# A soft mixture-of-experts product with two and three levels of fast matrix multiplication: products regrouped in pairs, more pairs split a third time, VectorE planned by other durations

## The chip, the cores and the metric

The kernel runs on one core of a Trainium2 chip. The metric is device time in microseconds (us) of one execution, from the host's view of the device; the profiler's span, from the first to the last instruction, is a little shorter. TensorE (PE) multiplies, VectorE (DVE) adds, subtracts and multiplies elementwise, ScalarE (ACT) copies, GpSimd (POOL) and SyncE (SP) do almost nothing here but start transfers (DMAs); ACT starts some too. Each of these engines works through its own queue in the order in which the program put the instructions there.

## What is computed

Every token gets a weight for each of 8 experts by a softmax, and the output is the weighted sum of the experts' products:

```
batch, seq, hidden, n_experts, expert_hidden = 16, 512, 512, 8, 2048
probs = softmax(router_logits)                       # [16, 512, 8]
for e in range(n_experts):
    output += probs[:, :, e:e+1] * np.matmul(x, expert_weights[e])
```

With the weights multiplied into x this is one product: 8192 tokens by a depth of 8 x 512 = 4096, times 4096 by 2048.

## The kernel before

**Three levels.** The product is split by Winograd's form of Strassen's scheme: seven half-size products in place of eight, for some additions of blocks. On the outer level tokens come in 16 pairs q of 256-token blocks (2q and 2q+1), the depth in two halves of 4 experts and the columns in two halves of 1024. The seven outer products are called 1, 2, 5, 6, 7, 4, 3 here (P1, P2, ...), in the order in which the kernel goes through them; each runs over all q (P1 from q = 2 on; what it would give for q = 0 and 1 is computed directly at the start). On the inner level each outer product is split again into seven **steps**, `STEPS = (1, 5, 6, 2, 7, 3, 4)`, each of 128 tokens, depth 1024 and 512 columns: eight matmuls of 512 columns. On the third level, in a **third** stage, the steps 1 and 5 of two outer products of one kind are taken together (256 tokens, depth 1024, 512 columns) and split into seven parts of four matmuls of 256 columns each, twice: 56 matmuls of 256 columns in place of 32 of 512.

**Stages and slots.** `stages` is a list of one or two outer products that run interleaved, step by step; a stage of two has 14 **slots** of one step each (`SLOT = 1.73`, the us that the plan takes for one). Stages 0 to 14 hold P1 and P2, `k5` = 15 is the first of P5. `run(stage)` goes through them; in a third stage `run_third` first runs the 14 parts, with the last two slots of the stage before put between them (`held`), and then slots 4 to 13. `at(stage, slot, ...)` hangs work on a slot: casts and fetches of weights, fetches of bases.

**What a step needs.** A left operand (`Left`): x times the probabilities, for both halves of depth (`times`, one DVE operation of 128x2048 each, written to a z tile), a difference `s2` (128x1024) and a difference `i` (128x2048). A right operand (`Right`): seven blocks of 1024 x 512 weights, of which four (5, 6, 7, 4) are differences (128x4096 on DVE). In a third stage four more sums `s` per stage (128x1024) and, once per kind of product, eight differences `t` of weights (`Split`, 128x1024 each). After a step the result leaves PSUM: `post_alone` (P1, P5, P3: two of seven copies add on DVE, the others are ACT copies) or `post_on_base` (P2, P6, P7, P4: six of seven add on DVE to a base already in an `h` tile). In a third stage there are four more half-width additions on DVE and four half-width copies on ACT, two of which write a temporary `t5` in an `h` tile.

**The order of DVE.** DVE's order is written out while the program is built. `later(cost, make)` appends an operation to one first-in-first-out `queue`; `slack()` after every slot advances a clock of PE by `SLOT` and takes operations from the queue as long as DVE's own clock is `LAG` = 0.3 behind it; `need` takes everything up to an operation that the next step needs; `evacuated` puts in an addition that reads PSUM. The costs are 0.69, 1.22, 2.29 and 0.42 us for 1024, 2048, 4096 columns and the half-width addition. At slot 1 of a stage the left operands of the next one are queued (`queue_lefts`), at its start the `i` of its own.

**Loads.** `start_loads(s + 2)` at slot 1 of stage s starts the loads of x and of the probabilities (`pT`), `finish_loads(s + 2)` at slot 7 turns x that was read for the first time (`xs`, cast by POOL) by four DMA transposes on SP's queue; its transposed form is stored for later use (`x_dram`, read back as `xT<-x`). `xpool` has 10 tiles of 2 KB per partition for these, `hpool` 12 tiles of 2 KB for outputs, bases and `t5`, `wpool` 15 tiles of 8 KB for weights, `t`, `s` and weights being prepared. P1's results for q go to `kept` in DRAM and are read again as P6's base, and as P2's where they are not in `h` tiles any more.

**Stages 0 to 14 before.** Four pairs of P1 (q = 2 to 9), six mixed stages of P2 with q = 9 to 14 and P1 with q = 10 to 15, five pairs of P2 (15, 0 to 8). Stages 2, 3 (P1) and 11 (P2) are third stages, and six of P3 at the end. In mixed stages P2 with q >= 9 takes its base and its transposed x from the tiles that P1 left.

**Weights for later.** `b21` is block 21 of the weights, cast in stages 0 to 2, from which P2's operands are made in stage 3. T blocks (`t1`, `t2`, `t3`: differences of blocks 11, 12 and 22) are made for three of four (k, n) by `wedge`, from `b11` in SBUF and two casts, in six halves in stages 4 to 9, and for `ODD` = (0, 1) by `odd_t` from three whole casts. They go to DRAM, `t1` and `t2` come back for P5 and P6.

**The end.** The last stage holds one product, P3 with q = 13, as `finish`, with steps 1, 5, 6, 7, 3, 4, 2; step 2 is computed in two halves of 256 columns at the very end, the first copied by DVE, the second by ACT.

Of the kernel before, what the change touches and what calls it, by code (L numbers as in the profile page):

```python
# [31 lines left out]
def kernel(  # L32
# [34 lines left out]
    xpool = ctx.enter_context(tc.tile_pool(name="xpool", bufs=10))  # L67
    hpool = ctx.enter_context(tc.tile_pool(name="hpool", bufs=12))
# [304 lines left out]
    def evacuated(cost=0.69):  # L373
        clock["dve"] = max(clock["dve"], clock["pe"]) + cost
# [51 lines left out]
    class Left:  # L426
# [31 lines left out]
        def queue_make(self, k):  # L458
            for make in self.makes(k):
                self.task[k] = later(1.22, make)  # L460

        def queue_s2(self):
# [3 lines left out]
            self.task["s2"] = later(0.69, make)  # L466

        def queue_i(self):
# [5 lines left out]
            self.task["i"] = later(1.22, make)  # L474
# [19 lines left out]
    class Right:  # L494
# [9 lines left out]
        def queue_sum(self, sums, p):  # L504
            self.task[p] = later(2.29, sums[p])
# [66 lines left out]
    class Split:  # L572
# [5 lines left out]
        def queue(self):  # L578
            for p in THIRD:
                for i in range(4):  # L580
                    self.task[p, i] = later(0.69, lambda p=p, i=i: self.make(p, i))
# [18 lines left out]
    class Third:  # L600
# [5 lines left out]
        def queue_sums(self):  # L606
            for i in range(4):
                self.task.append(later(0.69, lambda i=i: self.make(i)))
# [17 lines left out]
        def part(self, p, m):  # L626
# [14 lines left out]
            elif m in (6, 7):  # L641
                evacuated(0.42)
# [41 lines left out]
    right[1] = Right(w, {p: Task(2.29, sums[p]) for p in (6, 7, 4)})  # L684
# [33 lines left out]
    def product(r, q, **how):  # L718
# [7 lines left out]
        elif r == 2:  # L726
            if q >= 9:
# [111 lines left out]
    def run(stage):  # L839
# [3 lines left out]
        slots = [(p, i) for i in range(len(STEPS)) for p in some]  # L843
# [54 lines left out]
    def joined(q, tn):  # L898
        m1 = bases[6, q]
        m1.task[tn] = later(0.69, lambda: tt(m1.t[tn], m1.t[tn], products[5, q].o[tn], SUB), True)  # L900
# [40 lines left out]
    def wedge_at(stage, slot, kn, e, then):  # L941
# [7 lines left out]
        def go_on():  # L949
            for make in made:  # L950
                later(1.22, make)
# [8 lines left out]
    for i, kn in enumerate(((0, 0), (0, 1), (1, 1), (1, 0))):  # L960
        at((11 * i + 8) // 14, (11 * i + 8) % 14, lambda kn=kn: cast21(kn))
# [8 lines left out]
    sums_at(3, 3, 2, b21, (5,))  # L970
    sums_at(3, 5, 2, b21, (6,))
    sums_at(3, 7, 2, b21, (7,))
    sums_at(3, 12, 2, b21, (4,))
    for i, (kn, e) in enumerate((kn, e) for kn in ((0, 0), (1, 0), (1, 1)) for e in range(2)):
        wedge_at(4 + i, 2, kn, e, (4 + i, 11))
# [9 lines left out]
    def cast_odd(q):  # L985
        made[q] = cast_block(q, ODD)

    def odd_t():

        def make1():  # L990
            t1[ODD] = made[11]
            tt(t1[ODD], made[11], made[12], SUB)
# [221 lines left out]
```

## Time and profile before

| | us |
|---|---|
| median of 3 runs | 1382.1 |
| lowest, highest | 1379.82, 1384.07 |
| profiled execution, its time | 1378.23 |
| profiled execution, its span | 1376.5 |
| POOL queue's transfers | 185.12 MB |
| SP queue's transfers | 130.15 MB |
| ACT queue's transfers | 42.08 MB |

The profile is one execution on the chip. Times in its views are from the span's start. An instruction's duration includes its passage through the engine's pipeline, so that in a busy engine the next one starts before the first has ended; where the text speaks of **spacing** it means the difference of two starts. A number in brackets at the end of a row is the idle time of the engine before that instruction and what ended it. Almost every instruction goes through a helper, so rows are told apart by their tiles: `ps<-w,z` is an ordinary step, `ps<-w,d` is step 6, `ps<-t,s`, `ps<-w,s` and `ps<-t,z` are parts of the third level, `z<-xT,pT` makes a left operand, `z<-z,d` is an `i`, `h<-ps,h` an addition that empties PSUM.

### The profile page before, as it was taken

How to read it: one execution, taken by the hardware profiler on the slowest of the kernel's cores; microseconds unless marked ns; L12 is line 12 of the kernel's file. 1: busy time of each engine (PE TensorE's matmuls, PEld its weight loads, DVE VectorE, ACT ScalarE, POOL GpSimd, SP SyncE). 2: the span in 40 equal slices, each digit the busy share in tenths (PEclk: the TensorE clock that was granted, in tenths of full speed). 3: DMA queues.
4: the chain of work that ended last, by engine and by line, in shares of the span. 5: the costliest groups of instructions: out<-in, count | busy, mean ns of one | idle time of the engine just before them, and what ended most of it. 6: DMA issues, size and time to landing. Idle time of an engine off the chain costs nothing.

```text
span 1376.5 us, 18061 instructions
## 1 busy us (share of the span) xinstructions
PE 1363.1 (99%) x6610; PEld 643.8 (47%) x6610; DVE 1125.8 (82%) x1360; ACT 193.3 (14%) x353; POOL 411.4 (30%) x652
## 2 busy tenths in 40 slices
PE   8999999999999999999999999999999999999998
PEld 4455444445444444444444444444444444456554
DVE  5877767678989888789897878888889898987875
ACT  3222111100001111111111100000000000123221
POOL 3122333231222243343242112232332422232222
PEclk9999999999999999999999999999999999999999
DMA  9999899999897999999999898888797969999886
GB/s 180 199 258 219 214 233 279 236 315 340 252 327 237 321 308 315 295 318 320 334 286 307 327 399 237 194 236 211 227 266 203 259 188 310 289 225 239 211 184 117
DMA packets 193161, 358.50 MB, mean 260 GB/s; under 512 B 53168, under 2 KB 87216, under 8 KB 187696
## 3 DMA queue, kind: packets, MB, share of 16 engines
q0 software_dynamic: 88688, 185.12, 55.7%
q1 hardware_dynamic: 98336, 130.15, 31.1%
q10 hardware_dynamic: 6048, 42.08, 8.0%
q8 instruction: 51, 0.84, 0.2%
q14 instruction: 38, 0.31, 0.1%
HBM read 214.47 MB, written 170.07 MB: 279 GB/s over the span
## 4 chain that ended last, share of the span: by engine, by line
PE 69%; issue 11%; DMA 11%; POOL 5%; DVE 3%; SPq 1%; ACT 0%; POOLq 0%; DVEq 0%; ACTq 0%
PE ps L132 69%; POOL out_dram L126 3%; DMA out_dram<-h 3%; DMA wd<-w 2%; DMA w<-in_expert_weights_dram 2%; DMA w<-wd 2%; DMA xT<-xs 1%; POOL wd L126 1%; DMA pT<-p_dram 1%; SPq L397 1%; DVE h L112 1%; POOL w L126 1%; DVE z L112 1%; DVE s L112 0%; POOL xs L126 0%
## 5 line engine op out<-in xcount | busy, mean ns | idle before, releaser
L132 PE MATMUL ps<-w,z 128*128 128x512 f16 (+1 forms) x5272 | 1136.0, 376 | 3.8 <-DMA w<-in_expert_weights_dram 1.9
L132 PEld LDWEIGHTS <-z 128*128 128x128 f16 x5344 | 522.6, 98 | 609.6 <-issue 2.5
L126 POOL DMA_DIRECT2D out_dram<-h x380 | 248.6, 660 | 724.1 <-ACT h L559 352.2
L112 DVE TENSOR_TENSOR h<-ps,h 128x512 f32<-128x512 f32 x415 | 284.7, 688 | 175.0 <-PE ps L132 147.0
L112 DVE TENSOR_TENSOR z<-xT,pT 128x2048 f16<-128x2048 f16 x220 | 266.8, 1218 | 12.1 <-DMA xT<-xs 10.0
L132 PE MATMUL ps<-w,d 128*128 128x512 f16 x880 | 199.1, 379 | 1.2 <-DMA w<-wd 1.2
L132 PEld LDWEIGHTS <-d 128*128 128x128 f16 x880 | 86.1, 98 | 103.3 <-issue 1.5
L112 DVE TENSOR_TENSOR z<-z,d 128x2048 f16<-128x2048 f16 x110 | 132.3, 1217 | 0.0
L112 DVE TENSOR_TENSOR w<-w 128x1024 f16<-128x1024 f16 (+2 forms) x92 | 101.0, 1103 | 5.9 <-DMA wd<-w 3.4
L559 ACT COPY h<-ps 128x512 f32<-128x512 f32 x64 | 37.5, 586 | 482.9 <-PE ps L132 414.2
L548 ACT COPY h<-ps 128x512 f32<-128x512 f32 x90 | 52.7, 586 | 325.6 <-PE ps L132 304.6
L112 DVE TENSOR_TENSOR ps<-ps,h 128x512 f32<-128x512 f32 (+1 forms) x102 | 60.6, 599 | 31.9 <-PE ps L132 31.8
L112 DVE TENSOR_TENSOR d<-z 128x1024 f16<-128x1024 f16 x110 | 74.8, 686 | 2.0 <-PE ps L132 0.7
L545 ACT COPY h<-ps 128x512 f32<-128x512 f32 x90 | 52.0, 589 | 151.7 <-PE ps L132 146.6
L126 POOL DMA_DIRECT2D w<-in_expert_weights_dram x65 | 48.4, 761 | 38.6 <-DMA wd<-w 28.3
L126 POOL DMA_DIRECT2D wd<-w x86 | 48.2, 584 | 37.1 <-DVE w L112 28.9
L126 POOL DMA_DIRECT2D kept<-h x56 | 30.8, 550 | 73.8 <-ACT h L548 41.1
L112 DVE TENSOR_TENSOR z<-z,u 128x2048 f16<-128x2048 f16 x38 | 46.4, 1221 | 0.6
L112 DVE TENSOR_TENSOR u<-xT,pT 128x2048 f16<-128x2048 f16 x38 | 46.3, 1217 | 0.0
L112 DVE TENSOR_TENSOR h<-h 128x512 f32<-128x512 f32 (+2 forms) x69 | 45.2, 676 | 0.4 <-DMA h<-kept 0.3
L541 ACT COPY ps<-ps 128x512 f32<-128x512 f32 x45 | 25.6, 570 | 104.5 <-PE ps L132 99.4
L112 DVE TENSOR_TENSOR z<-z 128x2048 f16<-128x2048 f16 x32 | 39.1, 1222 | 0.6
(61 smaller groups left out, 262.5 us busy)
## 6 DMA issues: line engine op xcount, KB each, us to landing
out_dram<-h POOLq DMA_DIRECT2D x380, 256.0 KB, 6.7
pT<-p_dram SPq DMA_DIRECT2D x127, 256.0 KB, 6.3
w<-wd ACTq DMA_DIRECT2D x27, 1024.0 KB, 9.4
h<-kept SPq DMA_DIRECT2D x100, 256.0 KB, 7.1
xT<-x SPq DMA_DIRECT2D x74, 256.0 KB, 6.6
wd<-w POOLq DMA_DIRECT2D x72, 256.0 KB, 6.7
w<-in_expert_weights_dram POOLq DMA_DIRECT2D x35, 512.0 KB, 9.9
h<-out_dram SPq DMA_DIRECT2D x68, 256.0 KB, 4.8
```

The source lines that it names most:

```text
L112: dve(nc.vector.tensor_tensor(out=o, in0=a, in1=b, op=op))
L126: note(nc.gpsimd.dma_start(out=o, in_=i, **how))
L132: note(nc.tensor.matmul(ps, z, w, start=start, stop=stop, skip_group_check=True))
L397: note(nc.sync.dma_start_transpose(out=self.t[:, :, ds(j * P, P)], in_=self.xs[:, j, :]))
L541: act(nc.scalar.copy(self.banks["b"], x))
L545: act(nc.scalar.copy(o[tn], q if p == 5 else x))
L548: act(nc.scalar.copy(o[TN[p]], b if p == 2 else x))
L559: act(nc.scalar.copy(o[tn], b))
```

## The change

The stages 0 to 14 become seven pairs of P1 (q = 2 to 15) and eight of P2 (14 and 15, then 0 to 13), none mixed. Third stages are 2 to 6 (P1) and 8 to 11 (P2), nine where there were three; those of P3 stay. P2 takes base and x from the tiles of P1 for q = 14 and 15 alone. The casts of `b21` move to stages 3 to 5, P2's operands are made in stage 6. `wedge` makes T blocks for (0, 0) and (1, 0) in stages 1 to 5, during P1; for (1, 1) `odd_t` makes them in stages 7 to 9, during P2, from three whole casts, and `t1` of it stays in SBUF. DVE is planned with 0.61, 1.14, 2.2 and 0.35. `xpool` has 9 tiles and `hpool` 13. In the last stage step 3 stands before 7, and step 4 between the halves of step 2; both halves are copied by ACT.

```
-    xpool = ctx.enter_context(tc.tile_pool(name="xpool", bufs=10))
-    hpool = ctx.enter_context(tc.tile_pool(name="hpool", bufs=12))
+    xpool = ctx.enter_context(tc.tile_pool(name="xpool", bufs=9))
+    hpool = ctx.enter_context(tc.tile_pool(name="hpool", bufs=13))
...
-    def evacuated(cost=0.69):
+    def evacuated(cost=0.61):
...
-                self.task[k] = later(1.22, make)
+                self.task[k] = later(1.14, make)
...
-            self.task[p] = later(2.29, sums[p])
+            self.task[p] = later(2.2, sums[p])
...
-                evacuated(0.42)
+                evacuated(0.35)
...
-            if q >= 9:
+            if q >= 14:
                 base = products[1, q].o.__getitem__
...
-    for q in (2, 4, 6, 8):
+    for q in range(2, 16, 2):
         add(product(1, q), product(1, q + 1))
-    for q in range(9, 15):
-        add(product(2, q), product(1, q + 1))
-    forget(*range(0, 18, 2))
-    rest = [15] + list(range(9))
-    for i in range(0, 10, 2):
+    k2 = len(stages)
+    forget(*range(0, 28, 2))
+    rest = [14, 15] + list(range(14))
+    for i in range(0, 16, 2):
         k = add(product(2, rest[i]), product(2, rest[i + 1]))
         for slot, tn in zip((8, 10, 12, 13), INNER):
             for q in rest[i:i + 2]:
-                if q < 9:
+                if q < 14:
                     fetch_at(k if tn == (1, 0) else k - 1, 3 if tn == (1, 0) else slot, bases[2, q], tn)
...
-    for i, kn in enumerate(((0, 0), (0, 1), (1, 1), (1, 0))):
-        at((11 * i + 8) // 14, (11 * i + 8) % 14, lambda kn=kn: cast21(kn))
+    for where, kn in zip([(3, 10), (4, 7), (5, 4), (5, 13)], ((0, 0), (0, 1), (1, 1), (1, 0))):
+        at(*where, lambda kn=kn: cast21(kn))
...
-    sums_at(3, 3, 2, b21, (5,))
+    sums_at(k2 - 1, 3, 2, b21, (5,))
...
-    for i, (kn, e) in enumerate((kn, e) for kn in ((0, 0), (1, 0), (1, 1)) for e in range(2)):
-        wedge_at(4 + i, 2, kn, e, (4 + i, 11))
+    for (kn, e), (where, then) in zip(((kn, e) for kn in ((0, 0), (1, 0)) for e in range(2)), [((1, 2), (1, 13)), ((2, 4), (3, 1)), ((3, 6), (4, 3)), ((4, 8), (5, 5))]):
+        wedge_at(*where, kn, e, then)
...
+    for q, where in zip((12, 11, 22), [(7, 4), (7, 10), (8, 2), (8, 12)]):
+        at(*where, lambda q=q: cast_odd(q, (1, 1)))
+    at(*(8, 12), lambda: odd_t((1, 1)))
     for i, kn in enumerate(((0, 0), (1, 1), (1, 0))):
-        fetch_at_w(11 + (8 + 4 * i) // 14, (8 + 4 * i) % 14, t1, "t1", kn)
+        if kn != (1, 1):
+            fetch_at_w(11 + (8 + 4 * i) // 14, (8 + 4 * i) % 14, t1, "t1", kn)
...
-    finish.steps = (1, 5, 6, 7, 3, 4, 2)
+    finish.steps = (1, 5, 6, 3, 7, "2a", 4, "2b")
...
-    for stage in (2, 3):
+    for stage in [2, 3, 4, 5, 6]:
         third(stage, 1)
-    at(1, 2, splits[1].queue)
-    for stage in (11,):
+    at(1, 0, splits[1].queue)
+    for stage in [8, 9, 10, 11]:
         third(stage, 2)
-    at(10, 2, splits[2].queue)
+    at(k2, 2, splits[2].queue)
```

`splits[r].queue` puts the eight differences `t` into DVE's queue: before at slot 2, behind the next stage's left operands that come at slot 1; for P1 now at slot 0, ahead of them.

More of the change, by code (lines that the diff above doesn't have):

```diff
@@ L683 @@
     right = {r: Right() for r in (2, 5, 6, 7, 4, 3)}
-    right[1] = Right(w, {p: Task(2.29, sums[p]) for p in (6, 7, 4)})
+    right[1] = Right(w, {p: Task(2.2, sums[p]) for p in (6, 7, 4)})
     lefts, xs, ps_, bases = {}, {}, {}, {}
@@ L842, in run @@
             p.left.queue_i()
-        slots = [(p, i) for i in range(len(STEPS)) for p in some]
+        slots = [(p, i) for i in range(len(some[0].steps)) for p in some]
         def one(n):
```

82 lines of the change are left out of this document (44 added, 38 removed).

## The prediction

> **What bounds the kernel now.** I read the page's head first, then who PE waited for, then the order of time on PE, then DVE, ACT and SP around each place where PE stood.
>
> ```profile
> span 1376.5 us, 18061 instructions
> PE 1363.1 (99%) x6610; PEld 643.8 (47%) x6610; DVE 1125.8 (82%) x1360; ACT 193.3 (14%) x353; POOL 411.4 (30%) x652
> ...
> PE ps L132 <- DVE t L112: 1.3, 1, 1.3
> PE ps L132 <- DMA w<-wd: 1.2, 1, 1.2
> ```
>
> PE is the bound; it waits for single microseconds in single places. So the time falls if PE gets fewer columns, or if those places go, and rises if a cover breaks.
>
> ```profile
> 1153.03 3.62 PE L132 MATMUL ps<-w,d 128*128 128x512 f16 x16
> 1156.48 20.88 PE L132 MATMUL ps<-w,z 128*128 128x512 f16 x96
> 1177.20 3.62 PE L132 MATMUL ps<-w,d 128*128 128x512 f16 x16
> ...
> 1223.01 1.04 PE L132 MATMUL ps<-w,s 128*128 128x256 f16 x8
> ...
> 1224.76 3.62 PE L132 MATMUL ps<-w,d 128*128 128x512 f16 x16
> 1248.14 2.11 PE L132 MATMUL ps<-w,d 128*128 128x512 f16 x9
> ...
> L132 PEld LDWEIGHTS <-s 128*128 128x128 f16 x288 | 28.1, 98 | 8.4 <-issue 2.1 <-DVE s L112 1.3
> ```
>
> Step 6 (`ps<-w,d`) comes once per stage, so it is a ruler. An ordinary stage takes 1177.20 - 1153.03 = 24.17 us (16 matmuls 3.45, so 0.216 each), a third stage 1248.14 - 1224.76 = 23.38 (16 matmuls of 256 columns from 1223.01 on take 1.75, so 0.109 each, with the weight loads, 98 ns, hidden beside them). Check: 32 x 0.216 = 6.9 against 56 x 0.109 = 6.1, difference 0.8.
>
> **Six more third stages** (five of P1 for two, four of P2 for one; P3's six stay). Each saves 24.17 - 23.38 = 0.79: 6 x 0.79 = **-4.7 us**. It is PE's own work, so nothing hides it.
>
> The Trainium skill speaks against it: "TensorE: Matmul & The Clock Gate", section "Back-to-back issue gap", has the sustained spacing set by the weight load as well, 81 ns at 128 columns and 131 at 512. A straight line between gives an estimate of 98 at 256 columns, and then a third stage would cost 56 x 98 - 32 x 131 = 1.3 us instead of saving. The rows above disagree (109 and 216 ns).
>
> **The first third stage** (2, in both kernels).
>
> ```profile
> 74.73 3.62 PE L132 MATMUL ps<-w,d 128*128 128x512 f16 x16
> ...
> 79.34 1.23 DVE L112 TENSOR_TENSOR z<-xT,pT 128x2048 f16<-128x2048 f16 x1 [7.44 <-DMA xT<-xs]
> ...
> 86.74 0.69 DVE L112 TENSOR_TENSOR t<-w 128x1024 f16<-128x1024 f16 x1
> ...
> 91.34 2.76 PE L132 MATMUL ps<-w,z 128*128 128x512 f16 x16 [0.73 <-DVE h L112]
> ...
> 99.61 3.62 PE L132 MATMUL ps<-w,d 128*128 128x512 f16 x16
> ```
>
> DVE stood 7.44 us for a transposed x, and only then, at 86.74, came to the eight `t` that the third level needs; PE lost 1.5 by the ruler (99.61 - 74.73 = 24.88, less 23.38), half of it before 91.34. Queued at slot 0, the `t` (8 x 0.6 = 4.8) go into that 7.44. I take **-1.1**; bounds 0 (the x is later still) and -1.5. The wedge now at slots 2 and 13 of stage 1 is queued behind the next left operands, so it delays stage 3, which has room.
>
> **The first third stage of P2** (11 before, 8 after) shows what can go wrong four times.
>
> ```profile
> 292.21 3.62 PE L132 MATMUL ps<-w,d 128*128 128x512 f16 x16
> ...
> 293.80 0.69 DVE L112 TENSOR_TENSOR h<-ps,h 128x512 f32<-128x512 f32 x1 [2.94 <-DMA kept<-h]
> ...
> 300.94 2.36 DVE L112 TENSOR_TENSOR z<-xT,pT 128x2048 f16<-128x2048 f16 x2
> 303.21 0.69 DVE L112 TENSOR_TENSOR h<-ps,h 128x512 f32<-128x512 f32 x1
> 303.81 0.69 DVE L112 TENSOR_TENSOR t<-w 128x1024 f16<-128x1024 f16 x1
> ...
> 308.00 0.69 DVE L112 TENSOR_TENSOR t<-w 128x1024 f16<-128x1024 f16 x1
> 308.75 0.60 PE L132 MATMUL ps<-t,s 128*128 128x256 f16 x4 [1.26 <-DVE t L112]
> 311.86 0.60 PE L132 MATMUL ps<-w,z 128*128 128x256 f16 x4 [0.35 <-ACT ps L638]
> 311.16 0.37 ACT L640 COPY h<-ps 128x256 f32<-128x256 f32 x1 [3.66 <-DMA out_dram<-h]
> ...
> 317.51 3.62 PE L132 MATMUL ps<-w,d 128*128 128x512 f16 x16
> ```
>
> Spacings: 0.60 for 1024 columns and for an addition from PSUM (303.21 to 303.81), 2.27/2 = 1.13 for 2048. The new costs 0.61 and 1.14 are these; the old ones were 8 to 15% over. PE lost 317.51 - 292.21 - 23.38 = 1.9 here, for two things. First, the fifth `t` ended at 308.7. From the stage's start (292.21 less four slots, 285.3) DVE owes 2 `i` (2.3), 10 additions (6.0), 4 left halves (4.5), 4 `s` and 2 `s2` (3.6) and 5 `t` (3.0), in all 19.4, against 12 slots of 1.73 plus the parts ahead of it, 22.0; the idle 2.94 for a store that had not landed, with 0.5 for PE, used the room up. Secondly `t5` found all 12 `h` tiles taken and waited 3.66 for an output to land, with the next ACT copy behind it.
>
> In stage 7 DVE owes the same 19.4. The wait for `kept<-h` should shrink: stage 6 has no output stores and no weight casts ahead of it on POOL's queue. The 13th `h` tile gives the first `t5` its place, so the next ACT copy is not stuck. I put the stall at 0.7 (bounds 0 and 1.9), a gain of **-1.2**. Stages 8 to 10 owe from third to third 12 additions (7.2), 4 half-width ones (1.7 by the old plan's cost), 2 `i` (2.3) and 8.1 of left operands and sums, 19.3 of 23.4; 1.8 of late `t` and then 6.6 of `odd_t` (3 x 2.2, row below) come on top. `odd_t` is queued behind stage 10's left operands, so stage 9 is asked for 25.9 and about 2.5 spill into 10, 21.8 of 23.4: full, not over.
>
> ```profile
> 137.67 2.28 DVE L112 TENSOR_TENSOR w<-w 128x4096 f16<-128x4096 f16 x1
> 139.87 2.35 DVE L112 TENSOR_TENSOR z<-z,d 128x2048 f16<-128x2048 f16 x2
> ```
>
> "VectorE: DVE Perf Modes" of the Trainium skill, section "The DRAIN you can't avoid", lets the next operation start only when the pipeline is empty. By durations these stages would owe a tenth more and stage 9 would miss its end; starts 0.60 apart for 0.69 long say otherwise.
>
> **The end.**
>
> ```profile
> 1363.57 1.89 PE L132 MATMUL ps<-w,d 128*128 128x512 f16 x8
> ...
> 1365.50 0.69 DVE L112 TENSOR_TENSOR h<-ps,h 128x512 f32<-128x512 f32 x1 [1.03 <-DMA out_dram<-h]
> 1366.24 7.09 PE L132 MATMUL ps<-w,z 128*128 128x512 f16 x40 [0.78 <-DVE h L112]
> ```
>
> Alone in its stage, step 7 goes on in the bank that step 6 just filled, and waits for DVE to read it: 1366.24 - 1363.57 - 8 x 0.216 = 0.95. With step 3 (1.73) between, that read is covered. Step 4 has half of step 2 (0.87) between it and 7; a read of about 0.95 leaves 0.1. **-0.85**, bounds 0 and -0.95. The tail behind the last matmul is an ACT copy and its store in both: 0.
>
> **The new plan of DVE** holds for all stages. It pulls operations up to 8% earlier, into gaps such as this:
>
> ```profile
> 1327.17 0.69 DVE L112 TENSOR_TENSOR h<-ps,h 128x512 f32<-128x512 f32 x1 [1.82 <-issue]
> 1332.97 0.69 DVE L112 TENSOR_TENSOR s<-z 128x1024 f16<-128x1024 f16 x1
> 1333.71 0.61 PE L132 MATMUL ps<-t,s 128*128 128x256 f16 x4 [1.02 <-DVE s L112]
> ```
>
> Here DVE idled 1.82 and PE then lost 1.0. I count half, **-0.5**, bounds -1.0 and, where an operation pulled forward waits for its load with additions behind it, a loss of up to the 2.94 seen above. The price of an addition that comes up to 0.84 later (one 1.14 operation less LAG) is nothing in a stage of two, where a bank is next used three slots (5.2) on.
>
> **Loads and buffers.** P2's base and x for five more q are read back: 20 x 256 KB and 5 x 256 KB; the block 11 cast for (1, 1) replaces a store and a fetch of `t1`. They cost PE nothing while they land a stage ahead. A tile less in `xpool` bounds SP:
>
> ```profile
> SPq L123 <- DVE z L112: 414.5, 55, 21.1
> ...
> 889.59 1.81 SPq L123 DMA_DIRECT2D h<-out_dram  x4
> 891.45 0.42 SPq L123 DMA_DIRECT2D pT<-p_dram  x1
> 895.76 0.33 SPq L123 DMA_DIRECT2D xT<-x  x1
> ```
>
> SP issues when DVE releases a tile, two at a time here. With nine, each load takes the release after: nothing to speak of inside a couple, 4.3 us (891.45 to 895.76) across; the bases issued between shift by the same, and loads run a stage (24) ahead. P1's pairs turn two new x per stage for seven stages instead of four, with `b21` casts and wedges beside them in 3 to 5:
>
> ```profile
> 67.80:92.70 24.90, 24.17 (x120) 11.62 (x119) 15.97 (x22) 6.53 (x13) 5.16 (x8) 1.00 1.19 248
> 188.60:212.80 24.20, 24.20 (x114) 10.99 (x113) 16.75 (x20) 3.50 (x6) 8.22 (x15) 1.00 1.03 250
> ```
>
> The next to last column, the DMA share, is higher where two x are turned (1.19) than where one is (1.03). What more it costs no row shows. From below it is 0; from above the 7.44 wait of DVE, repeated in four stages against some 7 us of room (x came at 79.34 and, without the `t`, would have served until about 87), so 0 to 3 each. I take **+1.9** for this, for P2's full stages and for waits the new order brings.
>
> Sum: -4.7 - 1.1 - 1.2 - 0.85 - 0.5 + 1.9 = **-6.5**. The profiled execution took 1378.23 (span 1376.5 and 1.7 around it), so 1371.7 by its measure; the median of the three runs is 3.9 higher, 1382.1, and I state the forecast against that: **1375.6**.
>
> **Rivals.** (B) *Every P2 third stage stalls as stage 11 did*, 1.9 each: 7.6 instead of 0.7. For it: four full DVE stages, `h` tiles wanted 14 to 13. Against: half of that loss was a late store, and the 13th tile. 1375.6 + 6.9 = 1382.5: no change.
> (C) *P1's transposes fall behind*: two x per stage, one tile less and the casts beside them, so that from stage 3 on x lands later than some 9 us before the third stage begins. DVE waits first in line with wedge and sums behind it; 3 us in each of stages 3 to 6, 12 less the 1.9 already counted: 1385.7, slower; and P2's operands in stage 6 come late as well. Against: `b21` no longer competes in stages 0 to 2, and P1 asks DVE for 14.5 of 23.4 (4 left halves 4.5, 2 `i` 2.3, 2 `s2` and 4 `s` 3.6, 4 additions 2.4, half-width ones 1.7).
> (D) *The third level costs rather than saves*, where weight loads don't hide: 56 x (109 + 98) = 11.6 us against 32 x (216 + 98) = 10.0, so +1.6 for -0.79, six times: 1375.6 + 14.3 = 1389.9, slower. For it: the load is nine tenths of a 256-column matmul. Against: the third stages of P3 ran at 23.4. That is the way of the page on TensorE named above; the trace bears it out nowhere.
> (E) *The waits are many small ones*: 5.9 in place of my 1.9, of the kinds in B and C. 1379.6, no change to measure.
>
> **Chances.** Forecast 0.60, E 0.13, B 0.10, C 0.15, D 0.02. A difference under 0.3% (4.1 us) can't be told from none. Of the forecast's 0.60, 0.08 gains less than that; of E 0.05 and of B 0.03 gain more; of C 0.03 loses less. Faster 0.60 - 0.08 + 0.05 + 0.03 = 0.60; slower 0.15 - 0.03 + 0.02 = 0.14; same 0.26. The range reaches down to 1369.5 (all gains at their bounds, -4.7 - 1.5 - 1.9 - 0.95 - 1.0 = -10.1, so 1372.0, and 2.3 below it, as the lowest of the three runs lies below their median) and up to 1386, past C.
>
> **What would show it.** Right: step 6 spaced 23.38 in stages 3 to 6 and 9 to 11; no wait for `t` near 90; PE's stall at step 7 of the last stage gone; DVE starts unchanged. Wrong: PE waits on `DVE s`, `z` or `t` in stages 7 to 11 (B), DVE idle for `xT<-xs` of more than 7 us in stages 2 to 5 (C), new gaps after stage 15, where PE's work is unchanged.

## The result, and the profile after

| | before | after |
|---|---|---|
| median of 10 runs each, side by side (us) | 1381.18 | 1387.84 |
| lowest, highest | 1375.44, 1386.5 | 1384.05, 1392.29 |
| profiled execution: time, span | 1378.23, 1376.5 | 1387.86, 1385.3 |

The changed kernel is slower: ratio 1.0055 with a 95% interval of 1.0038 to 1.0071, some 6.7 us, where 6.5 us less were forecast. The time lies 1.8 us above the upper end of the range, between rivals C (1385.7) and D (1389.9); the ruler below tells these apart.

The head of the page of after, and its list of what PE waited for (engine, line and releaser: sum in us, times, longest):

```profile
span 1385.3 us, 18509 instructions
PE 1361.5 (98%) x6754; PEld 658.6 (48%) x6754; DVE 1145.0 (83%) x1404; ACT 201.0 (15%) x378; POOL 410.9 (30%) x650
...
PE ps L132 <- DVE h L112: 10.2, 4, 5.9
PE ps L132 <- ACT ps L638: 3.0, 1, 3.0
PE ps L132 <- DVE ps L112: 2.5, 4, 1.8
```

PE is busy 1.6 us less than before (1363.1), although its matmuls ran at half speed for some 5 us of it, as will be seen; the span is 8.8 longer. The gap is PE standing still, and the longest waits are for additions on DVE (`h`, `ps`), not for `t`, `s` or weights.

The ruler says where. PE's order of time in after, step 6 of stages 1 to 7, and the rows in which PE waited:

```profile
74.82 3.62 PE L132 MATMUL ps<-w,d 128*128 128x512 f16 x16
98.20 3.62 PE L132 MATMUL ps<-w,d 128*128 128x512 f16 x16
121.58 3.62 PE L132 MATMUL ps<-w,d 128*128 128x512 f16 x16
144.96 3.62 PE L132 MATMUL ps<-w,d 128*128 128x512 f16 x16
161.79 2.76 PE L132 MATMUL ps<-w,z 128*128 128x512 f16 x16 [1.10 <-DVE h L112]
...
171.04 1.03 PE L132 MATMUL ps<-t,z 128*128 128x256 f16 x8 [1.80 <-DVE ps L112]
171.91 3.62 PE L132 MATMUL ps<-w,d 128*128 128x512 f16 x16
...
193.53 5.04 PE L132 MATMUL ps<-w,z 128*128 128x512 f16 x16 [5.90 <-DVE h L112]
...
203.63 3.62 PE L132 MATMUL ps<-w,d 128*128 128x512 f16 x16
227.80 3.62 PE L132 MATMUL ps<-w,d 128*128 128x512 f16 x16
```

Stages 2, 3 and 4 are 23.38 apart to the hundredth: a third stage without a stall costs what the prediction said. Stage 5 took 171.91 - 144.96 = 26.95 and stage 6 203.63 - 171.91 = 31.72: losses of 3.6 and 8.3. The same subtraction over all stages (24.17 for an ordinary one, 20.72 and 15.54 for stages with one product at an edge) gives the account, in us lost against a stage without a stall:

| place | before | after |
|---|---|---|
| stage 2, first third stage | 1.5 | 0 |
| stages 5 and 6 | 0 | 11.9 |
| P2's third stages (11; 8 to 11) | 1.9 | 3.7 (stage 10 0.5, 11 3.2) |
| stages 15 to 53 | 1.5 (stage 32) | 4.7 (23 2.1, 27 2.0, 24 and 33 0.3 each) |
| stage 54, and the end | 1.2 + 0.95 | 0 + 0.1 |
| sum | 7.0 | 20.4 |

13.4 more lost, less 6 x 0.79 = 4.7 saved, is 8.7; the last matmuls of the two profiled executions lie 8.6 apart. (Before's profiled execution lies below its median, so that the medians differ by 6.7.) The account is of one execution of each, and losses of 1 to 5 us come and go between executions: the 1.5 of stage 2 did not come in experiment 2, which has that place as before.

**Stages 5 and 6.** The chain that ended last, over this stretch of after (start, length, what):

```profile
139.32 11.87 DMA xT<-xs
...
151.77 5.63 DMA xs<-in_x_dram
157.43 1.30 SPq L397
158.73 0.05 issue
158.78 10.56 DMA xT<-xs
```

This is a ring. A cast of x (`xs`, POOL) waits for a tile, which comes free when a transposition has landed; the transposition (SP) waits for the cast; with nine tiles the second product's transposition also waits for the tile of the first one's `xs`. So the steps run one after the other: 11.87 + 5.63 + 10.56 and the issues between, 30 us (139.3 to 169.3) in a stage of 23.4. The three engines show the same, each in its own order of time. SP's rows of the transpositions:

```profile
75.83 10.79 SPq L397 DMA_TRANSPOSE xT<-xs  x4
97.94 15.62 SPq L397 DMA_TRANSPOSE xT<-xs  x4
125.51 15.89 SPq L397 DMA_TRANSPOSE xT<-xs  x4
157.43 14.58 SPq L397 DMA_TRANSPOSE xT<-xs  x4
```

What SP's queue waited for in this stretch (60 to 210):

```profile
SPq L397 <- DMA xT<-xs: 35.4, 6, 9.9
```

What POOL's casts of x waited for, at the row 151.77 of the chain:

```profile
151.77 1.45 POOL L126 DMA_DIRECT2D xs<-in_x_dram  x2 [11.71 <-DMA xT<-xs]
```

DVE's left operands:

```profile
151.26 1.23 DVE L112 TENSOR_TENSOR z<-xT,pT 128x2048 f16<-128x2048 f16 x1 [7.42 <-DMA xT<-xs]
169.42 1.23 DVE L112 TENSOR_TENSOR z<-xT,pT 128x2048 f16<-128x2048 f16 x1 [1.81 <-issue]
183.01 1.23 DVE L112 TENSOR_TENSOR z<-xT,pT 128x2048 f16<-128x2048 f16 x1 [11.69 <-issue]
```

SP's rounds start 22, 28, 32 us apart, and within a round it waits for the first two to land before the others start: the lead of two stages is used up in stage 4, and in stage 6 DVE stands 11.69 us at the head of its queue with additions behind it. (That row names no releaser but "issue". The round's last transposition was issued at 170.71 and landed at 182.93, so this too is a wait for x.) A reader who looks at POOL sees the second half of the ring: for 11.71 us nothing leaves POOL's queue, neither the stores of `kept` nor the casts of `b21`.

And PE lost more than it waited. Two stretches of after by windows (length, busy us and instructions of PE, PEld, DVE, ACT, POOL, then PEclk, DMA share, GB/s):

```profile
187.00:193.50 6.50, 0.63 (x6) 0.41 (x5) 6.47 (x9) 1.15 (x4) 0.86 (x2) 0.84 1.02 348
193.50:198.00 4.50, 4.47 (x14) 1.90 (x14) 4.50 (x6) 0.59 (x1) 3.52 (x7) 0.50 0.97 377
```

After the pause, matmuls of 512 columns followed one another in 0.427 and those of 256 in 0.213 until 198.2, twice the ordinary 0.216 and 0.109. Of stage 6's 8.3 us some 6 are the pause and 2.3 the slow matmuls behind it.

**P2's third stages.** ACT's order of time in after:

```profile
318.60 0.37 ACT L640 COPY h<-ps 128x256 f32<-128x256 f32 x1 [4.95 <-DMA out_dram<-h]
```

The `t5` of stage 11 again found every `h` tile taken, 13 of them now. POOL's order of time shows the store that would free one, and the casts of weights ahead of it on the same queue:

```profile
293.98 1.53 POOL L126 DMA_DIRECT2D w<-in_expert_weights_dram  x2
...
300.23 0.56 POOL L126 DMA_DIRECT2D out_dram<-h  x1 [0.16 <-issue]
```

It landed at 318.5, 18.3 us later. PE's next `ps` waited 3.0 for it.

**P5 and P6 (from stage 15 on)**, where PE's work is the same in both kernels. DVE's order of time in after:

```profile
581.56 0.69 DVE L112 TENSOR_TENSOR h<-h 128x512 f32<-128x512 f32 x1 [3.47 <-DMA h<-kept]
...
682.49 0.69 DVE L112 TENSOR_TENSOR h<-h 128x512 f32<-128x512 f32 x1 [5.04 <-DMA h<-kept]
```

`joined`, the difference that makes P6's base, stood at the head of DVE's queue before what it reads had landed. The additions behind it came late, and PE lost 2.1 in stage 23 and 2.0 in 27.

**The end** went as forecast. In PE's order of time of after step 3 stands between 6 and 7, and no row there has a wait:

```profile
1373.01 1.89 PE L132 MATMUL ps<-w,d 128*128 128x512 f16 x8
1374.74 7.16 PE L132 MATMUL ps<-w,z 128*128 128x512 f16 x40
```

### The profile page after: what moved, and what is told of

Same layout as the page of the kernel before. It is cut to its first block, busy times and chain, and to the rows that moved or that the text cites. A ratio compares the mean times of both kernels' runs of the same rounds, so it can differ in the third digit from the quotient of the medians.

```text
span 1385.3 us, 18509 instructions
## 1 busy us (share of the span) xinstructions
PE 1361.5 (98%) x6754; PEld 658.6 (48%) x6754; DVE 1145.0 (83%) x1404; ACT 201.0 (15%) x378; POOL 410.9 (30%) x650
## 4 chain that ended last, share of the span: by engine, by line
PE 68%; DMA 13%; issue 12%; POOL 4%; DVE 1%; SPq 1%; ACT 0%; POOLq 0%; DVEq 0%; ACTq 0%
PE ps L132 68%; DMA xT<-xs 4%; DMA xs<-in_x_dram 3%; DMA out_dram<-h 2%; DMA w<-in_expert_weights_dram 1%; POOL out_dram L126 1%; POOL kept L126 1%; DMA wd<-w 1%; POOL w L126 1%; DMA x<-xT 1%; SPq L397 1%; POOL wd L126 1%; DVE h L112 0%; DVE z L112 0%; POOL xs L126 0%
## 5 line engine op out<-in xcount | busy, mean ns | idle before, releaser
L132 PE MATMUL ps<-w,z 128*128 128x512 f16 (+1 forms) x5176 | 1111.0, 374 | 15.2 <-DVE h L112 10.2
L112 DVE TENSOR_TENSOR ps<-ps,h 128x512 f32<-128x512 f32 (+1 forms) x126 | 69.7, 564 | 29.5 <-PE ps L132 29.4
L132 PEld LDWEIGHTS <-s 128*128 128x128 f16 x480 | 46.9, 98 | 9.0 <-issue 0.5
L132 PE MATMUL ps<-t,s 128*128 128x256 f16 x360 | 49.1, 273 | 0.2 <-DVE ps L112 0.2
```

The lines of the kernel that those rows point to most:

```text
L112: dve(nc.vector.tensor_tensor(out=o, in0=a, in1=b, op=op))
L132: note(nc.tensor.matmul(ps, z, w, start=start, stop=stop, skip_group_check=True))
```

## The experiments

What the trace suggests, with the letters of the expectations. T: x's way in P1 (nine tiles, two x turned per stage) stalls stages 5 and 6. W: it is the casts of T blocks and of `b21` beside it. O: the new plan of DVE makes the waits after stage 15. S: stage 11 waits for stores of P2 that lie behind casts on POOL's queue. Against all of them: the more third stages themselves cost the time. D in the expectations is no fixed theory; each says what it means by it. "Losses" are by the ruler, of the profiled execution.

**1. The two pools as before.** The changed kernel with

```
-    xpool = ctx.enter_context(tc.tile_pool(name="xpool", bufs=9))
-    hpool = ctx.enter_context(tc.tile_pool(name="hpool", bufs=13))
+    xpool = ctx.enter_context(tc.tile_pool(name="xpool", bufs=10))
+    hpool = ctx.enter_context(tc.tile_pool(name="hpool", bufs=12))
```

> The changed kernel with xpool 10 and hpool 12 again, all else as changed. DVE's order is the same. Theory T (the tile taken from xpool makes the second x of a P1 pair wait for the first one's transposes, so that a round of cast, four transposes and landing takes 27 to 32 us, longer than the 23.4 of a third stage): the rounds fall back to at most 24 us, step 6 is spaced 23.4 to 24 in stages 5 and 6 (26.9 and 31.7 in the changed kernel), the waits for h<-kept near 578 and 677 go, and the time is 10 to 16 us below the changed kernel's 1387.8, so 1372 to 1378. Rival D (two new x per stage with casts beside them are too much for the DMA whatever the pool holds): stages 5 and 6 stay above 26, the time within 4 us of 1387.8. Stage 11 may lose more than its 3.1, with one h tile less.

1382.92, ratio to before 1.0033 (1.0009 to 1.0057). SP's rows:

```profile
75.81 5.44 SPq L397 DMA_TRANSPOSE xT<-xs  x4
96.71 7.08 SPq L397 DMA_TRANSPOSE xT<-xs  x4
121.24 7.07 SPq L397 DMA_TRANSPOSE xT<-xs  x4
153.10 9.98 SPq L397 DMA_TRANSPOSE xT<-xs  x4
```

The first three rounds are issued in half the time, the transpositions no longer wait for `xT<-xs` on SP's queue (the loads and stores of the queue still do), and stages 5 and 6 lose 1.3 and 3.4 in place of 3.6 and 8.3. But the round at 153.10 is still late, and T had expected 10 to 16 us less: against the kernel before run beside each, the ratio fell from 1.0055 to 1.0033, some 3 us, with intervals that overlap. The tenth tile is not the whole of it. Experiments 6 and 7 are the same kernel as this one up to stage 9, and there stages 5 and 6 lost 7.2 and 8.5 together, so the tile is worth between 3.4 and 7.2 of after's 11.9 in these stages.

**2. The two pools alone, on the kernel before.**

```
-    xpool = ctx.enter_context(tc.tile_pool(name="xpool", bufs=10))
-    hpool = ctx.enter_context(tc.tile_pool(name="hpool", bufs=12))
+    xpool = ctx.enter_context(tc.tile_pool(name="xpool", bufs=9))
+    hpool = ctx.enter_context(tc.tile_pool(name="hpool", bufs=13))
```

> The kernel of before with xpool 9 and hpool 13, nothing else. T: P1's stages 0 to 3, which turn two x each, and P5's, which turn one, wait as the changed kernel does; waits for h<-kept of 3 to 5 us on DVE after stage 20, a time 3 to 8 us above before's. D: no difference over 0.3%, apart from up to 1.9 gained in stage 11 by the 13th h tile.

1380.64, ratio 1.0011 (0.9993 to 1.0028): no difference that can be told. T had expected 3 to 8 us more. Stages 1 to 3, which need two new x each and have casts of `b21` beside them but no wedge, lost nothing, and neither did the mixed stages with one new x each: there nine tiles do. Stage 11 lost 1.5, behind a late `t` (PE waited 1.33); its `t5` found a tile among the 13 at once.

**3. The new costs alone, on the kernel before**: in `evacuated` and wherever `later` has a cost,

```
-    def evacuated(cost=0.69):
+    def evacuated(cost=0.61):
...
-                self.task[k] = later(1.22, make)
+                self.task[k] = later(1.14, make)
...
-            self.task[p] = later(2.29, sums[p])
+            self.task[p] = later(2.2, sums[p])
...
-                evacuated(0.42)
+                evacuated(0.35)
```

> The kernel of before with DVE's costs 0.61, 1.14, 2.2 and 0.35, nothing else. T: the new order is harmless, within 0.3% of before, the 1.0 us wait for s in the last third stage gone. Rival O (operations pulled forward wait for loads, and the additions behind them with them, which made the stalls near 585 and 684): waits for h<-kept on DVE of 3 to 5 us after stage 20 and a time 2 to 5 us above before's.

1385.75, ratio 1.0041 (1.0017 to 1.0064). Stages 32 and 54 lose nothing now, as hoped, but stage 23 loses 5.2 and 33 2.2. DVE's rows there:

```profile
576.84 0.69 DVE L112 TENSOR_TENSOR h<-h 128x512 f32<-128x512 f32 x1 [4.01 <-ACT h L545]
...
590.67 1.42 DVE L112 TENSOR_TENSOR w<-w 128x1024 f16<-128x1024 f16 x2 [3.40 <-DMA wd<-w]
```

and PE's:

```profile
581.18 8.79 PE L132 MATMUL ps<-w,z 128*128 128x512 f16 x40 [1.57 <-DVE h L112]
592.74 7.50 PE L132 MATMUL ps<-w,z 128*128 128x512 f16 x34 [2.76 <-DVE h L112]
```

The cost of the new plan alone is shown by the runs, 0.4%. The rows show how: planned as cheaper, `joined` and the differences `w<-w` come in DVE's order before what they wait for (a copy of ACT, a store that frees their tile) is done, and the additions behind them come late. The costs are nearer to the measured spacings, yet the old ones held a margin.

**4. The old costs in the changed kernel**: experiment 1 with experiment 3's lines the other way round.

> The changed kernel with xpool 10, hpool 12 and DVE's old costs. T: as with the pools alone within 3 us, the wait for s in the last third stage back (1 us). O: 2 to 5 us better than with the pools alone. If P2's third stages need the new order, stalls in stages 8 to 11 grow by some us.

1391.5, ratio 1.0075 (1.0046 to 1.0104), 8.6 above experiment 1: losses 5.1, 3.9, 4.9 and 2.3 in stages 5, 6, 11 and 12. O had expected 2 to 5 us less, and it missed: with the old costs too stages 23, 24 and 32 lost 2.5, 1.7 and 1.5, hardly less than with the new ones in experiment 1 (5.8 against 6.4 in stages 15 to 53). So the costs can't be judged alone: DVE's full third stages seem to need the new ones.

**5. `b21` later.** Experiment 1 with its four casts behind the last x:

```
-    for where, kn in zip([(3, 10), (4, 7), (5, 4), (5, 13)], ((0, 0), (0, 1), (1, 1), (1, 0))):
+    for where, kn in zip([(4, 9), (5, 2), (5, 7), (5, 13)], ((0, 0), (0, 1), (1, 1), (1, 0))):
```

> pools_back with the four casts of b21 at (4, 9), (5, 2), (5, 7) and (5, 13) instead of (3, 10), (4, 7), (5, 4) and (5, 13), so that none stands ahead of the last pair's casts of x on POOL's queue. Theory T2 (what is left of the stalls in stages 5 and 6, 1.3 and 3.4, is x cast late behind weight casts in the same queue): the 13 us from issue to the transposes of stage 6's x fall to 8, stage 6 loses under 1, the time is 2 to 4 us below pools_back's 1382.9. Rival D2 (the transposes are slow because so much is in flight on the DMA engines as a whole): stage 6 still loses 2 to 4.

1382.66, ratio 1.0024 (1.0004 to 1.0043). Stages 5 and 6 lose nothing in this execution, 7 and 8 lose 2.7 and 4.5. In stage 7 DVE waited 6.4 for `wd<-w` and 1.5 for a cast before differences that make P2's operands; ahead of stage 8's loss it waited 4.2 for `xT<-xs` once more. The waits moved by two stages. Experiment 8 has the same casts and lost 4.6 and 1.7 in stages 5 and 6 all the same, so T2 is not shown.

**6. The old costs from P5 on** (experiment 1).

```
+    OLD = {0.61: 0.69, 1.14: 1.22, 2.2: 2.29, 0.35: 0.42}
+    as_before = [False]
+
+    def planned(cost):
+        return OLD[cost] if as_before[0] else cost
...
-        t = Task(cost, make)
+        t = Task(planned(cost), make)
...
+        as_before[0] = k >= k5
```

> pools_back with DVE's old costs from stage 15 on (P5 to the end), the new ones before that. Theory O (the new order of DVE makes the stalls in stages 23 and 33, 4.0 and 2.0 in pools_back, 5.2 and 2.2 in before_new_costs): both under 1, the waits for s in the last third stage (1.2) and near 804 to 813 (1.5) back, net 2 to 4 us below pools_back. Rival A (stage 23 stalls by the moved arrival of stores and weights in P5, which the new P1 and P2 bring along): 2 to 5 us stay in stages 23 and 24, the time within 2 us of pools_back.

1383.84, ratio 1.0037 (1.0019 to 1.0054). None of the stages 15 to 53 lost anything in this execution, as O has it; stage 54's 1.2 is back, and stage 6 lost 7.2. The time is not below experiment 1's, so the median doesn't show it. Nor do the traces one by one, since experiment 4 lost 5.8 in these stages with the old costs. PE's work in stages 15 to 53 is the same in all 18 profiled kernels: the nine with the old costs there lost 2.8 in the mean (0.1 to 7.8), the nine with the new ones 6.2 (0.9 to 11.4). Stage 54 lost 1.2 in all of the former and nothing in all of the latter.

**7. The casts of 11 and 22 for (0, 1) a stage later** (experiment 1).

```
-    for stage, slot, q in ((9, 9, 12), (10, 2, 11), (10, 9, 22), (last2, 8, 21)):
+    for stage, slot, q in ((9, 9, 12), (11, 2, 11), (11, 9, 22), (last2, 8, 21)):
...
-    at(11, 6, odd_t)
+    at(12, 6, odd_t)
```

> pools_back with the casts of blocks 11 and 22 for (0, 1) at (11, 2) and (11, 9) instead of (10, 2) and (10, 9), and their T blocks queued at (12, 6) instead of (11, 6). Theory S (the t5 copy of stage 11 waits for an h tile whose store stands behind 4 MB of weight reads in POOL's queue): the loss in stage 11 falls from 2.5 to under 0.7, that in stage 12 (0.9) too; 2 to 3 us less. Rival N (12 h tiles are too few for a P2 third stage whatever the casts do): stage 11 stays within 1 of 2.5.

1381.95, ratio 1.0018 (0.999 to 1.0045). Stage 11's 2.5 and stage 12's 0.9 are gone, and no `t5` waits for a tile: S is shown, by the trace and not by the median. Stages 5, 6 and 23 lost 5.7, 2.8 and 6.8 in this execution.

**8. Experiments 5, 6 and 7 together.**

> The three together: b21_after_x, old_costs_from_p5 and odd_casts_later on pools_back. If T2, O and S all hold, PE loses under 3 us beyond the startup and the time is 1372 to 1377, below both kernels; if the rivals hold, 1379 to 1384.

1380.21, ratio 1.0008 (0.9991 to 1.0024). No difference to before, where 1372 to 1377 were expected; the rivals' range (1379 to 1384) came. The ratio is 0.25% below experiment 1's, with intervals that overlap. Stages 15 to 53 lose 0.3 and the `t5` of stage 11 finds its tile, but stages 5, 6, 8, 9 and 11 still lose 4.6, 1.7, 4.3, 1.6 and 1.1.

**9. No transpositions.** The changed kernel, x cast straight into the tile of its transposed form; the transposition of x is left out.

```
-                self.xs = xpool.tile([P, HQ // P, H], f16, name="xs", tag="x")
-                pool(self.xs, x_f[ds(self.h * HQ, HQ), :].rearrange("(j p) h -> p j h", p=P))
+                self.t = xpool.tile([P, C, HQ], f16, name="xT", tag="x")
+                pool(self.t.rearrange("p (j c) t -> p j (c t)", j=HQ // P),
+                     x_f[ds(self.h * HQ, HQ), :].rearrange("(j p) h -> p j h", p=P))
+                self.new = True
```

> The changed kernel (pools 9 and 13) with the transposition of x left out: POOL casts new blocks of x straight into the tile from which left operands are made, so that a new x needs one tile and one transfer, no transposes on SP. Theory D (P1's pairs stall because the way of x, tile, cast, four transposes and landing, takes longer per pair than a third stage of 23.4): stages 5 and 6 lose under 0.5 where the changed kernel lost 3.6 and 8.3, and the waits for h<-kept behind transposes in P5 (stages 23, 27) shrink; 10 to 14 us less, 1374 to 1378. Rival W (the casts of weights and the stores beside them hold up P1, not x): stages 5 and 6 keep at least half of their 11.9.

1374.34, ratio 0.9975 (0.9963 to 0.9988). By the ratios that is 0.8% or some 11 us below after, with no loss in stages 2 to 9 but 0.4 in stage 6: the third stages of P1 do save what was said, once x is there. (A new x takes one tile here in place of two, so this edit also loosens the ring of tiles.)

**10. No wedge casts** (experiment 1). The eight casts of half blocks for the T blocks of (0, 0) and (1, 0) are left out, and these are made of block 11 alone.

```
-            cast_w(12, kn, e, a)
-            cast_w(22, kn, e, b)
+            pass
...
-            tt(u, b, a, SUB)
+            tt(u, b11[kn][:, rows, :], b11[kn][:, rows, :], SUB)
```

> pools_back with the eight casts of 512 KB for the T blocks in stages 1 to 4 left out (the T blocks are then made from block 11 alone; DVE's operations and the stores stay). W: stages 5 and 6, 4.7 in pools_back, lose under 1. D: they lose 3 or more.

1377.99, ratio 0.9993 (0.9971 to 1.0015). Stages 5 and 6 lose nothing. So taking away *either* load, transpositions or casts, is enough; W holds as much as T. The windows over stages 3 and 4 of experiment 1, in the order of the columns above (the DMA share is the sum of the packets' times over 16 engines, so it can pass 1):

```profile
92.70:116.10 23.40, 23.40 (x139) 13.31 (x137) 18.57 (x23) 6.94 (x14) 9.02 (x15) 1.00 1.10 251
116.10:140.30 24.20, 24.20 (x146) 14.02 (x145) 18.74 (x24) 6.94 (x14) 9.97 (x17) 1.00 1.15 265
```

and of this kernel:

```profile
92.70:116.10 23.40, 23.40 (x138) 13.30 (x136) 18.48 (x23) 6.95 (x14) 7.44 (x13) 1.00 0.81 244
116.10:140.30 24.20, 24.20 (x146) 13.97 (x143) 18.48 (x23) 7.51 (x15) 9.01 (x15) 1.00 0.83 228
```

DVE and PE do the same work here; the DMA share falls from 1.10 and 1.15 to 0.81 and 0.83. With it falls the time that a transposition takes from issue to landing: for those issued between 60 and 180 us its median is 8.3 in after and 7.8 in experiment 1, but 2.8 here and 2.5 in experiment 12. (In before it is 7.7; but from 102 us on a round there turns one x, so it has the time.)

**11. Fewer third stages in P1** (experiment 1).

```
-    for stage in [2, 3, 4, 5, 6]:
+    for stage in [2, 3]:
         third(stage, 1)
```

> pools_back with third stages 2 and 3 alone in P1 (4, 5 and 6 are ordinary ones). D with a way of x of some 24 us per pair: each of the three stages takes 0.79 more, but the stalls of 4.7 fall to under 1.5, so 1 us less to 1 more than pools_back. If the way takes much more than 24, the stalls stay above 3 and the time rises by 1 to 3.

1391.43, ratio 1.0094 (1.0067 to 1.0122). By the ratios that is some 8 us above experiment 1, of which the three ordinary stages explain 2.4; the rest is not explained (four runs). Ordinary stages give each x 0.8 us more, and stage 6 still lost 7.2. So the third level of stages 4 to 6 is not what P1's stalls come from.

**12. Nine tiles without the wedge casts.** Experiment 10 with the pools of the changed kernel, the last question about stages 5 and 6.

> The changed kernel, with its 9 buffers for x and 13 for h, without the eight casts of the four early T blocks (kn (0,0) and (1,0)): those casts and the two differences that follow them are left out, and what is made of them with it. Theory 'joint load' (x's way and the casts share POOL's queue; the ninth buffer matters only when they collide): stages 5 and 6 lose at most 1 us together as they did with ten buffers, 1377 to 1379. Theory 'ninth buffer' (nine buffers alone put a transposition behind the landing of the one before): stages 5 and 6 still lose 3 us or more together, 1381 or above.

1375.33, ratio 0.9975 (0.9963 to 0.9986). SP's rows:

```profile
76.07 6.31 SPq L397 DMA_TRANSPOSE xT<-xs  x4
96.39 6.63 SPq L397 DMA_TRANSPOSE xT<-xs  x4
120.41 6.40 SPq L397 DMA_TRANSPOSE xT<-xs  x4
148.71 6.74 SPq L397 DMA_TRANSPOSE xT<-xs  x4
```

With nine tiles the four are issued as fast as with ten, and stages 5 and 6 lose nothing. Two x per stage on nine tiles alone cost nothing; with the casts and ten tiles they cost 4.7 to 8.5 in these stages (experiments 1, 6 and 7), with the casts and nine tiles 11.9. By the ratios leaving out the casts is worth some 11 us with nine tiles and 5.5 with ten. That settles it as a joint overload, in which nothing is lost in these stages without the casts, and the missing tile makes the loss larger.

**13. Three edits on the kernel before**: the changed kernel's end, its `splits[1]` at (1, 0), and experiment 7's casts. This kernel leaves out the last half of step 2 in the last stage.

```
-    finish.steps = (1, 5, 6, 7, 3, 4, 2)
+    finish.steps = (1, 5, 6, 3, 7, "2a", 4, "2b")
...
-    at(1, 2, splits[1].queue)
+    at(1, 0, splits[1].queue)
```

> The kernel of before with three parts alone: the new order of steps at the end, the first t of P1 queued at slot 0 of stage 1, and the casts for (0, 1) at (11, 2) and (11, 9) with their T blocks at (12, 6). Its mixed stages, pools and costs are as before. By the places where PE stood in before: 1.5 in stage 2, 1.9 in stage 11 and 0.95 at the end go, 4.3 in all: 1374 to 1376, below both kernels. If the losses move elsewhere, within 0.15% of before.

1377.46, ratio 0.9993 (0.998 to 1.0007), with 0.87 us of work less. Stage 2 and the end lost nothing, stage 11 1.5 and stage 23 2.5.

**14.** The same with the whole of step 2:

> The kernel before with three edits that its stages or the changed kernel's speak for: the end's order of steps with the last one in two halves (stage 54's 0.95 us of waiting at the end, before 0.85 in the sum of the prediction), the right operand's third parts queued at (1,0) in place of (1,2) (stage 2's 1.5 us), and the odd block's casts 11 and 22 a stage later (stage 11's 1.9 us). Nothing is left out this time. If the losses are each their own: 1381.2 - 0.9 - 1.5 - 1.9 = 1376.9, ratio 0.997. If they are given back at the next wait (stage 32, stage 54, the joined differences): 1379 or above, ratio 0.998 to 1.

1377.49, ratio 0.9988 (0.9975 to 1.0001), 12 runs against 28: 1 us less by the medians, and not told from none. Stage 2's 1.5 and the end's 0.95 are gone in the profiled execution; stage 11 still lost 1.2, behind a late `t` (PE waited 1.06); its `t5` no longer waits. What is saved shows in the trace, and little of it in the median.

**15 and 16. One more third stage of P2 on the kernel before**, with the end's order and `splits[1]` at (1, 0): stage 12, as below, and in its place stage 13.

```
-    for stage in (11,):
+    for stage in (11, 12):
         third(stage, 2)
```

> The kernel before with the end's order and the third parts at (1,0) as in the run above, the odd block's casts as before, and one more stage split a third time, stage 12, which holds two products of P2. By the ruler one third stage saves 0.79: 1381.2 - 0.9 - 1.5 - 0.8 = 1378.0 if stage 11's loss stays at 1.9. If a second third stage in a row costs DVE its lead, stage 12 loses 1 us or more and it is 1379 or above.

> As the run above with stage 13 in place of 12, so that an ordinary stage lies between the two third stages. 1378.0 by the ruler; below the run above by 1 us or more if it is the lead of DVE that a third stage uses up, the same within 1 us if not.

1383.56, ratio 1.0036 (1.0022 to 1.005), and 1385.21, ratio 1.0044 (1.0028 to 1.0059). The added third stage, a gain of 0.79 by the ruler, cost 5 us or more, with an ordinary stage between as well as without. The second median lies 1.65 above the first; for DVE's lead as the cause it should have lain 1 us or more below. DVE's rows of the first:

```profile
344.75 4.61 DVE L112 TENSOR_TENSOR w<-w 128x4096 f16<-128x4096 f16 x2
349.28 2.35 DVE L112 TENSOR_TENSOR z<-z,d 128x2048 f16<-128x2048 f16 x2
```

PE's:

```profile
350.55 1.89 PE L132 MATMUL ps<-w,z 128*128 128x512 f16 x4 [2.99 <-DVE z L112]
```

and its windows from there on:

```profile
350.50:353.60 3.10, 3.05 (x8) 1.10 (x9) 2.26 (x2) 0.00 (x0) 0.00 (x0) 0.50 0.74 270
353.60:360.00 6.40, 6.40 (x31) 2.89 (x30) 5.59 (x8) 0.00 (x0) 1.63 (x3) 1.00 0.79 223
```

In this trace DVE has no room left beside `odd_t` (the 4.61 us), the `i` behind it is late, PE stands 2.99 and then pays half of that again at half clock: 4.6 in stage 13. In the changed kernel, with the new costs, the `odd_t` of (1, 1) at the end of stage 8 was followed by losses of 0 and 0.5.

## Why the prediction was wrong, point by point

- **Six more third stages, -4.7: right.** 23.38 apart wherever nothing stalls, and experiments 9 and 12, which leave out transpositions or casts, stand 3 us below before with all of them.
- **The first third stage, -1.1: right, and the bound (-1.5) was reached.** With the `t` at slot 0 stage 2 lost nothing, in after and in all 14 other kernels that have them there. In part this may be luck: with the `t` at slot 2 it lost 1.5 in before and 0.9 in experiment 3, but nothing in experiment 2.
- **P2's first third stage, -1.2 with a stall of 0.7 left: the stall stayed, in another stage.** Stage 8 lost nothing and 11 lost 3.2. The reason given, that the 13th `h` tile gives the first `t5` its place, held on the kernel before (experiment 2) and fell in the changed one: there the thirteen were taken as well, and what counts is when stores land behind casts (experiment 7). Rival B, four stalls of 1.9, did not come; experiments 15 and 16 show that its mechanism is there all the same.
- **The end, -0.85: right** (0.9).
- **The new plan of DVE, -0.5: the sign was wrong.** The stall of stage 54 that it was to shorten went in every trace, 1.2, and that of stage 32 in after, but 4.7 came in stages 23 to 33. Alone it costs 0.4% (experiment 3); stalls of this kind come with the old costs too, less in the mean (experiment 6). The upper bound, one wait of 2.94, was of the right kind, an operation pulled ahead of its load; it comes more than once, and I gave it no weight.
- **Loads and buffers, +1.9: here the prediction failed.** Stages 5 and 6 alone lost 11.9. Two steps of this term were wrong. The first is the price of two x per stage with casts beside them, for which "no row shows" what it costs, set at 0 to 3 a stage and 1.9 in all: with ten tiles the runs showed 4.7 to 8.5 in stages 5 and 6, and nothing once the wedge's casts were left out. The second is "with nine, each load takes the release after: nothing to speak of inside a couple", worth another 3.4 to 7.2 beside the casts. It was read off loads that DVE releases (P6 to P3, where x comes back from DRAM). In P1 a tile is released by a landing, the landing waits for a cast, and the cast for a tile, so a tile less makes work in parallel into work in series when the landings are slow, some 30 us a round where a stage has 23.4. Rival C named the place and the casts and put 12 on it. That 12 is near the 11.9 is luck: it was 3 in each of stages 3 to 6, and the loss came as 3.6 and 8.3 in two; P2's operands, which C had late, were in time. C had a chance of 0.15 because I weighed DVE's room (14.5 of 23.4) against it. DVE had that room. The ring runs over SP, POOL and the DMA engines. The DMA share, 1.19 against 1.03, which I quoted and then said that no row priced, pointed there, but it is a hint only: before has 1.07 between 92.7 and 116.1 us, and experiment 10 has 1.08 between 140.3 and 188.6, both without a stall. The rest of the miss is smaller: P2's third stages lost 1.7 more where 1.2 less was forecast, and stages 15 to 54 some 2 more where 0.5 less was.
- **A slip in the range.** Its lower end of 1369.5 does not follow from its own figures, 1372.0 less 2.3, which is 1369.7. Nothing hangs on it.
- **What would show it.** "DVE idle for `xT<-xs` of more than 7 us in stages 2 to 5" and "new gaps after stage 15" were the marks named for wrong, and both are there: 7.42 in stage 5 (11.69 came a stage later), and 23 to 33.

What stays open: how much of the loss with ten tiles belongs to the casts of `b21` (experiment 5 lost nothing in stages 5 and 6, experiment 8 with the same casts 6.3), which rows of DVE the new plan should leave where they were, and whether the casts can be put where neither x nor P2's operands wait; no such order was run. Experiment 14 is the only version whose median lies below the kernel before with nothing left out, by less than can be told.

## What to carry to other kernels

Before a pool loses a buffer, ask who releases it: where the release is a landing that itself waits for a buffer of the same pool, one less can turn overlap into a chain, and the chain's sum against the stage's length is the price; here that took a load which slowed the landings. A stage that is regrouped needs a budget for its DMA queues as much as for the vector engine: here eight casts beside two x per stage cost some 11 us with nine tiles. A planner's costs that lie above the measured spacings may be the margin that keeps operations behind the loads, copies and stores that they wait for: correct them together with the due times of those, and try that alone first.

## What the runs showed of the hardware that was not expected

A pause of PE costs more than itself. Over the profiles of all kernels here, from 40 us on, each of the 12 pauses of more than 3.35 us between two matmul starts was followed by matmuls at half speed (0.427 for 512 columns) for about 2.5 to 5.1 us; of 15 between 2.6 and 3.35 five were, the others not; of those between 2 and 2.6 none was. The profile's PEclk of 0.50 in the windows above (193.5 to 198.0 of after, 350.5 to 353.6 of experiment 15) says that it is the granted clock. The Trainium skill describes this: "TensorE: Matmul & The Clock Gate", section "What's actually happening", has the clock halved after an idle window of about 3.4 us that runs freely, and restored after about as long a busy one. The traces agree above 3.4 us and in the time until full speed is back; but five shorter pauses, from 2.68 us on, were followed by half speed too, and a whole idle window of 3.4 us doesn't fit into those. So a stall of some 3 us in a kernel bound by PE has two prices: stage 11 lost 3.2 in after with a pause of 3.28, and 4.7 in experiment 10 with one of 3.11 and slow matmuls behind it. The pause of 6.17 in stage 6 of after cost 8.3.
